# Turning the triangular blocks of a chunked delta-rule scan: products with the identity on TensorE in place of stream transposes on VectorE

## The chip, the cores and the metric

The kernel runs on one core of one Trainium2 chip. The metric is the device time of one launch in microseconds (us). Beside it stands the span of a profiled launch, from its first to its last instruction. TensorE (PE) runs at 2.4 GHz or at 1.2 GHz, as the chip grants; the profile shows the share granted, 1.00 or 0.50, or a mean of the two over a stretch.

## The reference

Two token streams (128 context tokens, 512 latent tokens) pass through two layers with shared weights. A layer mixes tokens in three ways, merges the three by gates, and ends in a feed-forward block. The change concerns one of the three, a chunked gated delta rule with 8 heads, a forward and a backward scan, and chunks of 64 tokens:

```python
    decay = jnp.exp(jnp.where(incl, gc[..., :, None] - gc[..., None, :], -jnp.inf))
    kb = k * beta[..., None]
    a_low = jnp.where(strict, jnp.einsum('bhnid,bhnjd->bhnij', kb, k) * decay, 0.0)
    m = a_low + jnp.eye(CHUNK, dtype=a_low.dtype)
    u = lax.linalg.triangular_solve(m, v * beta[..., None], left_side=True, lower=True, unit_diagonal=True)
    w = lax.linalg.triangular_solve(m, kb * jnp.exp(gc)[..., None], left_side=True, lower=True, unit_diagonal=True)
    ...
    def step(s, inp):
        u_n, w_n, qk_n, qg_n, kg_n, gl_n = inp
        v_new = u_n - jnp.einsum('bhcd,bhde->bhce', w_n, s)
        o = jnp.einsum('bhcd,bhde->bhce', qg_n, s) + jnp.einsum('bhij,bhje->bhie', qk_n, v_new)
        s = s * gl_n[..., None, None] + jnp.einsum('bhcd,bhce->bhde', kg_n, v_new)
        return s, o
```

Each chunk of each head and direction has a unit triangular 64x64 matrix `m`. The kernel inverts these matrices; the inverse then serves every product of the scan.

## The kernel before

**Data.** Activations lie transposed: channels on the 128 partitions, the 640 tokens along the row. The dense layers are *wide products*, 128x128 by 128x320. A float32 weight is split into a rounded part and a rest, and so are the activations, so that each 128x128 block of weights gives three products, written to a PSUM tile `pg`.

**Order of the work.** A recording layer writes one fixed order of instructions for each engine. The dense layers are the foreground. Everything else is a coroutine (`bg`), and `pump` (line 427), called between groups of wide products, steps those whose next work is due by an estimated clock that `tick` (line 365) keeps for each engine. A `yield` ends a step; its value says how many us ahead of its data a step may be issued. `finish_one` (line 448) steps a coroutine when the foreground has to wait for it. On the chip each engine then keeps to its order: an instruction that waits holds up everything behind it on its engine.

**The scans.** `delta` (line 1426) works on *units*: one chunk pair of 128 tokens, 8 heads, one direction in each half of the partitions. There are three sets of units for each layer (`batches`, line 1432): a *mixed* set of two units with both directions in each half (the context tokens), and two *plain* sets of four units (the latent tokens, directions 0 and 1). For each set, `prep` (line 1443) makes the matrices (`delta_unit`, line 1192: the decay from GpSimd and ScalarE, then 32 products of 64x64 for each unit on TensorE, and four VectorE multiplications) and inverts them (`delta_inv`, line 1229). Then `scan` (line 1465) runs the set's units one after another (`delta_step`, line 1346).

**The inverse** (`delta_inv`). `N`, seen as `Nm[partition, matrix, column]`, holds up to 32 matrices of 64x64 in each half of the partitions. Each matrix has two triangular 32x32 diagonal blocks, so the 128 partitions are four *quads* of 32 (`p` the half, `a` the block in it). In four parts:

- forward turn (`pack`, line 1244): from matrix layout (partition = row, and the 32 matrices side by side) to row layout in `U` (partition = matrix, and the 32x32 block along the row). A VectorE stream transpose turns 32 blocks of 32x32 of one quad; 4 for a plain set. In the mixed set the two directions need different layouts, so each quad is turned in both and the two are added, which takes 8 and one addition.
- the *substitution loop* (line 1265): 31 steps, on VectorE alone, 110 multiplications and subtractions that bring the inverse of all blocks into `X`.
- back turn (`unpack`, line 1279): `X` to matrix layout, back into `N` and, for one block of each matrix, the transposed block into `B`. 6 stream transposes for a plain set, 8 and 12 small copies for the mixed set.
- the off-diagonal block (from line 1305): two rounds of 32x32 products on TensorE, ScalarE takes their results out of PSUM.

`ident` is a 128x128 identity in the tile `small`. PSUM tiles `ps` (line 335) come from a pool of five. The tiles that the order and the rows call `A` are a shared pool: `N`, `U`, `X` and `B` are parts of `A` tiles.

Of the kernel before, what the change touches and what calls it, by code (L numbers as in the profile page):

```python
# [13 lines left out]
ALU = mybir.AluOpType  # L14
# [284 lines left out]
class _Net:  # L299
# [929 lines left out]
    def delta_inv(self, N, us):  # L1229

        nc = self.nc
        v = nc.vector
        nu = len(us)
        mixed = len(set(us)) > 1
        Nm = N.rearrange("p u c i -> p (u c) i")
        S = self.A()
        U = S[:, 0:1024].rearrange("p (r c) -> p r c", c=32)
        X = S[:, 1024:2048].rearrange("p (r c) -> p r c", c=32)
        tmp = S[:, 2048:2560]
        nc.gpsimd.memset(S[:, 1024:2048], 0.0)  # L1240
        nc.gpsimd.memset(S[:, 1024:2048].rearrange("p (r c) -> p r c", c=32).rearrange("p r c -> p (r c)")[:, 0:1024:33], 1.0)
        quads = [(p, a) for p in range(2) for a in range(2)]

        def pack(dst, p, a, bwd):
            q = slice(64 * p + 32 * a, 64 * p + 32 * a + 32)
            src = Nm[q, :, 32 * a:32 * a + 32].rearrange("p m i -> p i m")
            d = dst[q] if bwd else dst[q].rearrange("p r c -> p c r")
            v.transpose(out=d, in_=src)

        if not mixed:  # L1250
            for p, a in quads:
                pack(U, p, a, p ^ us[0])
                yield 1.5
        else:
            U2 = X
            for p, a in quads:
                pack(U, p, a, 0)
                yield 1.5
                pack(U2, p, a, 1)
                yield 1.5  # L1260
            v.tensor_tensor(out=U, in0=U, in1=U2, op=ALU.add)
            nc.gpsimd.memset(S[:, 1024:2048], 0.0)
            nc.gpsimd.memset(S[:, 1024:2048][:, 0:1024:33], 1.0)
        yield 1.5
        for c in range(31, 0, -1):
            js = [(c, 32)] if c > 24 else [(c, c + (32 - c) // 2), (c + (32 - c) // 2, 32)]
            tv = []
            for a, b in js:
                w = b - a
                tv.append(tmp[:, 256 * len(tv):256 * len(tv) + c * w].rearrange("p (r c) -> p r c", c=w))  # L1270
                v.tensor_tensor(out=tv[-1], in0=U[:, 0:c, c:c + 1].to_broadcast([P, c, w]),
                                in1=X[:, c:c + 1, a:b].to_broadcast([P, c, w]), op=ALU.mult)
            for (a, b), t in zip(js, tv):
                v.tensor_tensor(out=X[:, 0:c, a:b], in0=X[:, 0:c, a:b], in1=t, op=ALU.subtract)
            if c % 2 == 0:
                yield 1.5
        B = S[:, 0:1024].rearrange("p (m c) -> p m c", c=32)

        def unpack(dst, p, a, o2):
            q = slice(64 * p + 32 * a, 64 * p + 32 * a + 32)  # L1280
            src = X[q].rearrange("p r c -> p c r") if not o2 else X[q]
            v.transpose(out=dst.rearrange("p m i -> p i m"), in_=src)

        for p, a in quads:
            q = slice(64 * p + 32 * a, 64 * p + 32 * a + 32)
            bwd = p ^ us[0]
            nd = Nm[q, :, 32 * a:32 * a + 32]
            if mixed:
                unpack(nd, p, a, 0)
                yield 1.5  # L1290
                unpack(B[q], p, a, 1)
                ub = [u for u in range(nu) if p ^ us[u]][0]
                b3 = X[q, 0:8]
                bv, nv = B[q, ub * 8:ub * 8 + 8], nd[:, ub * 8:ub * 8 + 8]
                v.tensor_copy(b3, nv)
                v.tensor_copy(nv, bv)
                v.tensor_copy(bv, b3)
            else:
                unpack(nd, p, a, bwd)
                if a == bwd:  # L1300
                    yield 1.5
                    unpack(B[q], p, a, 1 - bwd)
            yield 0 if (p, a) == quads[-1] else 1.5

        W = S[:, 1024:2048].rearrange("p (m c) -> p m c", c=32)
        for m0 in range(0, nu * 8, 16):
            ps = self.ps()
            for m in range(m0, m0 + 16):
                s = us[m // 8]
                for p in range(2):  # L1310
                    fi = p ^ s
                    q0 = 64 * p + 32 * fi
                    q1 = 64 * p + 32 * (1 - fi)
                    nc.tensor.matmul(ps[q1:q1 + 32, (m - m0) * 32:(m - m0) * 32 + 32],
                                     Nm[q0:q0 + 32, m, 32 * (1 - fi):32 * (1 - fi) + 32], B[q0:q0 + 32, m],
                                     start=True, stop=True)
            for mm in range(m0, m0 + 16, 8 if mixed else 16):
                n = 8 if mixed else 16
                s = us[mm // 8]
                for p in range(2):  # L1320
                    q1 = 64 * p + 32 * (1 - (p ^ s))
                    nc.scalar.copy(W[q1:q1 + 32, mm:mm + n].rearrange("p m c -> p (m c)"),
                                   ps[q1:q1 + 32, (mm - m0) * 32:(mm - m0 + n) * 32])
        yield
        for m0 in range(0, nu * 8, 16):
            ps = self.ps()
            for m in range(m0, m0 + 16):
                s = us[m // 8]
                for p in range(2):
                    fi = p ^ s  # L1330
                    q0 = 64 * p + 32 * fi
                    q1 = 64 * p + 32 * (1 - fi)
                    nc.tensor.matmul(ps[q0:q0 + 32, (m - m0) * 32:(m - m0) * 32 + 32], W[q1:q1 + 32, m],
                                     Nm[q1:q1 + 32, m, 32 * (1 - fi):32 * (1 - fi) + 32], start=True, stop=True)
            for mm in range(m0, m0 + 16, 8 if mixed else 16):
                n = 8 if mixed else 16
                s = us[mm // 8]
                for p in range(2):
                    fi = p ^ s
                    q0 = 64 * p + 32 * fi  # L1340
                    nc.scalar.activation(Nm[q0:q0 + 32, mm:mm + n, 32 * (1 - fi):32 * (1 - fi) + 32],
                                         ps[q0:q0 + 32, (mm - m0) * 32:(mm - m0 + n) * 32].rearrange(
                                             "p (m c) -> p m c", c=32), AF.Copy, scale=-1.0)
        yield
# [857 lines left out]
```

## Time and profile before

| | us |
|---|---|
| time, median of 3 runs (lowest, highest) | 2847.31 (2843.88, 2851.53) |
| the profiled launch: its time | 2847.94 |
| its span | 2846.2 |
| TensorE busy | 2595.5 (91%) |
| VectorE (DVE) busy | 1870.7 (66%) |
| ScalarE (ACT) busy | 1030.8 (36%) |
| GpSimd (POOL) busy | 1331.2 (47%) |

The scans of layer 0 lie at about 290 to 610 us of the span, those of layer 1 at about 1690 to 2000 us. The busy shares are means over stages with different limits, so a stage is read by its own window. "Busy" of TensorE counts a product from its start to its modelled end; a product that runs at 1.2 GHz, or one that runs alone, counts for longer. The rate of a run of products is therefore read from the spacing of their starts. A float32 product stands as two matmul records in the trace.

### The profile page before, as it was taken

To read this page: it belongs to the slowest core of one execution; us is meant where nothing else is said; L and a number is where in the kernel's file an instruction comes from. 1 tells how busy PE (TensorE), PEld (TensorE's weight loads), DVE (VectorE), ACT (ScalarE), POOL (GpSimd) and SP (SyncE) were. 2 spreads that over 40 slices of the span, in tenths; PEclk is the share of its full clock that TensorE was granted. 3 is DMA by queue.
4 is the path that set the end of the run, shared out by engine and by line. 5 is a ranking of instruction groups with operands and counts; after the bars stand their busy time and mean duration, and the time that the engine had idled before them with its cause. 6 is when DMAs were issued, how large, how long until landed. Compare 5 with 4: busy or idle time off the path is not lost. (4 is left out here: it accounts for less than half of the span.)

```text
span 2846.2 us, 56258 instructions
## 1 busy us (share of the span) xinstructions
PE 2595.5 (91%) x22664; PEld 2455.5 (86%) x22664; DVE 1870.7 (66%) x3504; ACT 1030.8 (36%) x2235; POOL 1331.2 (47%) x1228
## 2 busy tenths in 40 slices
PE   5798879898999999999988988799899999999998
PEld 3677778898999989999987777688889989999997
DVE  4466897844654585667765779876556457877765
ACT  2445223332233243344425542333323323444432
POOL 1242535333334465566633444354423345767662
PEclk9899989999999999999999999899999999999999
DMA  7432122243564336422222322213336442222222
GB/s 277 165 99 93 61 85 66 78 139 120 186 241 135 112 98 202 139 83 82 82 99 80 108 85 72 78 57 97 109 140 232 157 163 62 73 82 82 82 75 82
DMA packets 99957, 324.24 MB, mean 114 GB/s; under 512 B 10842, under 2 KB 25178, under 8 KB 93216
## 3 DMA queue, kind: packets, MB, share of 16 engines
q1 hardware_dynamic: 98256, 312.76, 33.2%
q0 software_dynamic: 1440, 7.87, 0.8%
q8 instruction: 179, 2.93, 0.4%
q14 instruction: 82, 0.67, 0.1%
HBM read 288.60 MB, written 37.24 MB: 114 GB/s over the span
## 5 line engine op out<-in xcount | busy, mean ns | idle before, releaser
L2151 PE MATMUL pg<-A,wh 128*128 128x320 f32 (+1 forms) x6304 | 1477.1, 321 | 53.7 <-DVE T L2151 14.8
L2151 PEld LDWEIGHTS pg<-A,wh 128*128 128x128 f32 (+1 forms) x6304 | 1081.6, 194 | 107.5 <-issue 22.3
L2151 POOL TENSOR_TENSOR wl<-wr,wh 128x512 fp32r<-128x512 f32 (+2 forms) x486 | 677.5, 1407 | 777.5 <-ACT wh L2151 745.4
L2151 PE MATMUL pg<-A,wl 128*128 128x320 f32 (+1 forms) x3152 | 997.9, 317 | 0.5 <-POOL wl L2151 0.4
L2151 PEld LDWEIGHTS pg<-A,wl 128*128 128x128 f32 (+1 forms) x3152 | 610.7, 194 | 3.6 <-POOL wl L2151 2.6
L2151 ACT CAST wh<-wr 128x512 fp32r<-128x512 f32 (+2 forms) x486 | 286.7, 612 | 416.1 <-PE pg L2151 306.7
L2151 PE MATMUL ps<-A,wh 128*128 128x320 f32 x1696 | 379.6, 310 | 0.0
L2151 PEld LDWEIGHTS ps<-A,wh 128*128 128x128 f32 x1696 | 283.4, 188 | 3.4 <-issue 2.4
L2151 PE MATMUL ps<-A,wl 128*128 128x320 f32 x848 | 263.6, 311 | 4.6 <-POOL wl L2151 4.3
L2151 PE MATMUL ps<-A,A 32*32 32x32 f32 (+5 forms) x2984 | 214.0, 249 | 51.7 <-DVE A L2151 50.0
L2151 POOL TENSOR_TENSOR wl<-U,wh 128x512 fp32r<-128x512 f32 x160 | 225.9, 1425 | 52.9 <-ACT wh L2151 52.9
L2151 PEld LDWEIGHTS ps<-A,A 32*32 32x32 f32 (+2 forms) x2984 | 185.4, 152 | 63.8 <-DVE A L2151 51.2
L2151 DVE TENSOR_TENSOR A<-A 128x120 f32<-128x120 f32 (+22 forms) x690 | 215.6, 376 | 10.5 <-DMA A<-hyS 7.6
L2151 DVE TENSOR_TENSOR T<-T,T 128x320 f32<-128x320 f32 (+1 forms) x139 | 133.4, 960 | 100.6 <-ACT T L2151 96.4
L2151 POOL TENSOR_TENSOR A<-A,A 128x640 fp32r<-128x640 f32 (+5 forms) x84 | 121.4, 1457 | 113.3 <-ACT A L2151 110.0
L2151 PE MATMUL pg<-A,A 128*128 128x320 f32 x1056 | 164.6, 313 | 6.2 <-ACT A L2151 5.7
L2151 PEld LDWEIGHTS ps<-A,wl 128*128 128x128 f32 x848 | 159.6, 188 | 7.2 <-POOL wl L2151 7.2
L2151 PEld LDWEIGHTS pg<-A,A 128*128 128x128 f32 x1056 | 158.0, 190 | 8.5 <-ACT A L2151 6.0
L2151 ACT CAST wh<-U 128x512 fp32r<-128x512 f32 x160 | 99.1, 621 | 153.8 <-PE pg L2151 59.9
L2151 DVE STREAM_TRANSPOSE A<-A 32x1024 f32<-32x1024 f32 x72 | 149.0, 2093 | 1.3
L2151 DVE TENSOR_TENSOR U<-ps,U 128x512 f32<-128x512 f32 x144 | 78.1, 543 | 102.9 <-PE ps L2151 64.7
L2151 POOL TENSOR_TENSOR A<-U,A 128x320 fp32r<-128x320 f32 (+1 forms) x48 | 53.8, 1127 | 165.1 <-ACT A L2151 165.1
(166 smaller groups left out, 3120.1 us busy)
## 6 DMA issues: line engine op xcount, KB each, us to landing
wr<-in_wbig_dram SPq DMA_DIRECT2D x272, 512.0 KB, 3.7
A<-in_wmod_dram SPq DMA_DIRECT2D x96, 512.0 KB, 4.4
A<-hT SPq DMA_DIRECT2D x32, 1024.0 KB, 8.7
kSp<-U SPq DMA_DIRECT2D x40, 256.0 KB, 2.1
U<-kSp SPq DMA_DIRECT2D x40, 256.0 KB, 9.1
hyS<-T SPq DMA_DIRECT2D x24, 320.5 KB, 3.1
wr<-in_wbig_dram SPq DMA_DIRECT2D x16, 384.0 KB, 3.1
T<-hyS SPq DMA_DIRECT2D x16, 320.5 KB, 5.7
```

Of the source, the lines that this page charges most:

```text
L2151: return f(*a, **k)
```

## The change

In `delta_inv` every stream transpose becomes a group of float32 products on TensorE. The stationary operand is one strided column of `Nm` (32 matrices, 256 bytes apart) or one row or column of `X` (contiguous, or 128 bytes apart), the moving operand is the 32x32 identity of the quad, and the result, the block turned, lands in PSUM. ScalarE copies it from there to `U`, to `N` or to `B`. The four quads' products stand one after another, each on its own 32x32 block of TensorE.

- Plain set: forward 2 x 64 products and 4 copies; back 2 x (64 + 32) products and 12 copies.
- Mixed set: forward 2 x 64 products and 2 copies, and VectorE adds the second layout straight from PSUM in two halves; back 256 + 128 products with 8 moving columns and 8 copies. The 12 small VectorE copies and the second clearing of `X` on GpSimd go.
- The `yield 1.5` between the transposes go; a bare `yield` stands behind each group of products.

```diff
+        turn = lambda out, x, q, n: nc.tensor.matmul(out, x, self.ident[q, n], start=True, stop=True)
...
-            src = Nm[q, :, 32 * a:32 * a + 32].rearrange("p m i -> p i m")
-            d = dst[q] if bwd else dst[q].rearrange("p r c -> p c r")
-            v.transpose(out=d, in_=src)
...
-            v.tensor_tensor(out=U, in0=U, in1=U2, op=ALU.add)
-            nc.gpsimd.memset(S[:, 1024:2048], 0.0)
-            nc.gpsimd.memset(S[:, 1024:2048][:, 0:1024:33], 1.0)
+        for i0 in (0, 16):
+            ps = self.ps()
+            for i in range(16):
+                for p, a, q in quads:
+                    turn(ps[q, 32 * i:32 * i + 32], Nm[q, :, 32 * a + i0 + i], q, q)
+            v3 = ps.rearrange("p (i j) -> p i j", j=32)
+            if mixed:
+                nc.scalar.copy(U[:, i0:i0 + 16], v3)
+            else:
+                for p in range(2):
+                    h = slice(64 * p, 64 * p + 64)
+                    d = U[h, i0:i0 + 16] if p ^ us[0] else U[h, :, i0:i0 + 16].rearrange("p r c -> p c r")
+                    nc.scalar.copy(d, v3[h])
+            pss.append((i0, v3))
+            yield
+        if mixed:
+            for i0, v3 in pss:
+                d = U[:, :, i0:i0 + 16].rearrange("p r c -> p c r")
+                v.tensor_tensor(out=d, in0=d, in1=v3, op=ALU.add)
...
-            v.transpose(out=dst.rearrange("p m i -> p i m"), in_=src)
...
+                for i in range(ni):
+                    for p, a, q in quads:
+                        for u in range(nu) if mixed else (0, ):
+                            bwd = p ^ us[u]
+                            if o2 and a != bwd:
+                                continue
+                            m = slice(8 * u, 8 * u + 8) if mixed else slice(0, 32)
+                            x = X[q, i0 + i] if bwd ^ o2 else X[q, :, i0 + i]
+                            turn(v3[q, i, m], x, q, slice(q.start + m.start, q.start + m.stop))
...
+                    nc.scalar.copy(d.rearrange("p m i -> p i m"), v3[q, :, m])
+                yield
```

**VectorE, layer 0, start of the mixed set's inverse.** `A_2453` holds `N`, `A_2682` holds `U` and `X` of the mixed set; `A_2692` and `A_2693` belong to the first plain set. Before:

```order
L2151 TENSOR_TENSOR A_2453<-ps_2632,A_2453 128x256
L2151 STREAM_TRANSPOSE A_2682<-A_2453 32x32x32
L2151 STREAM_TRANSPOSE A_2682<-A_2453 32x1024
L2151 STREAM_TRANSPOSE A_2682<-A_2453 32x32x32
L2151 STREAM_TRANSPOSE A_2682<-A_2453 32x1024
L2151 STREAM_TRANSPOSE A_2682<-A_2453 32x32x32
L2151 STREAM_TRANSPOSE A_2682<-A_2453 32x1024
L2151 STREAM_TRANSPOSE A_2682<-A_2453 32x32x32
L2151 STREAM_TRANSPOSE A_2682<-A_2453 32x1024
L2151 TENSOR_TENSOR A_2682<-A_2682 128x1024
L2151 TENSOR_TENSOR A_2693<-ps_2788,A_2692 128x256
```

Now:

```order
L2157 TENSOR_TENSOR A_2453<-ps_2632,A_2453 128x256
L2157 TENSOR_TENSOR A_2682<-A_2682,ps_2685 128x16x32
L2157 TENSOR_TENSOR A_2682<-A_2682,ps_2769 128x16x32
L2157 TENSOR_TENSOR A_2682<-A_2682 128x31 x2
L2157 TENSOR_TENSOR A_2682<-A_2682 128x60
```

The eight transposes and the long addition are gone. Two additions that read PSUM stand in front of the substitution loop (the last two rows), and they need the products and copies of the two other engines first.

**TensorE, layer 0, end of the mixed set's inverse.** `ps_3869` is the first round of 32x32 products for the off-diagonal block, the first TensorE instruction that needs the substitution loop. Before:

```order
L2151 MATMUL pg_3862<-A_465,wh_3716 128x320
L2151 MATMUL pg_3862<-A_463,wl_3717 128x320
L2151 MATMUL ps_3869<-A_2682,A_2453 32x32 x32
L2151 MATMUL pg_3862<-A_463,wh_3716 128x320
L2151 MATMUL pg_3862<-A_465,wh_3716 128x320
```

Now the first that needs it are the 256 products of the back turn:

```order
L2157 MATMUL pg_3597<-A_465,wh_3440 128x320
L2157 MATMUL pg_3597<-A_463,wl_3441 128x320
L2157 MATMUL ps_3604<-small,A_2682 32x8 x256
L2157 MATMUL pg_3597<-A_463,wh_3440 128x320
L2157 MATMUL pg_3597<-A_465,wh_3440 128x320
```

Before, 534 wide products stand between the mixed set's units and `ps_3869`. Now 240 stand between its units and `ps_3604`, 228 of them behind the first group of forward turns. Wide products have moved from ahead of the inverse to behind it: up to the end of the last set's inverse there are 1778 before and 1610 now.

## Rows read from the trace of the kernel before

**Rows 1.** Windows: layer 0's and layer 1's inverses, then layer 0's three parts.
```profile
core 0: us, PE busy (x) PEld busy (x) DVE busy (x) ACT busy (x) POOL busy (x), PEclk, DMA share, GB/s
294.76:565.40 270.64, 227.40 (x3135) 215.04 (x3133) 234.64 (x481) 82.81 (x197) 121.79 (x151) 0.89 0.22 68
1693.07:1958.94 265.87, 223.88 (x3134) 212.04 (x3133) 232.04 (x481) 80.49 (x195) 125.30 (x148) 0.90 0.23 70
...
294.76:413.49 118.73, 90.66 (x790) 86.42 (x789) 116.53 (x241) 28.85 (x67) 50.67 (x65) 0.90 0.23 73
413.49:495.60 82.11, 76.17 (x1553) 70.11 (x1554) 56.94 (x104) 32.49 (x83) 47.23 (x60) 0.87 0.21 63
495.60:565.40 69.80, 60.56 (x793) 58.51 (x792) 61.17 (x138) 21.47 (x48) 23.89 (x26) 0.90 0.21 67
```

**Rows 2.** Groups of VectorE and TensorE, 294.76:565.40 (busy, mean ns | idle before <-releaser).
```profile
L2151 DVE TENSOR_TENSOR A<-A 128x126 f32<-128x126 f32 (+24 forms) x331 | 92.1, 342 | 1.5
L2151 DVE STREAM_TRANSPOSE A<-A 32x1024 f32<-32x1024 f32 x36 | 74.4, 2092 | 0.7
L2151 DVE SCALAR_TENSOR_TENSOR T<-T,par,T 128x641 f32<-128x641 f32 x24 | 30.0, 1251 | 16.1 <-POOL wl L2151 6.4 <-POOL A L2151 4.8 <-issue 4.3
L2151 DVE TENSOR_TENSOR A<-ps,A 128x256 f32<-128x256 f32 x32 | 12.7, 420 | 0.8 <-PE ps L2151 0.3
L2151 DVE COPY A<-A 32x256 f32<-32x256 f32 x12 | 4.5, 379 | 0.4
...
L2151 PE MATMUL pg<-A,wh 128*128 128x320 f32 x714 | 170.6, 328 | 8.9 <-DVE T L2151 8.8
L2151 PE MATMUL ps<-A 64*64 64x64 f32 x448 | 16.5, 224 | 4.0 <-DVE A L2151 3.0 <-DVE S L2151 1.1
L2151 PE MATMUL ps<-A,A 32*32 32x32 f32 x640 | 16.4, 222 | 24.4 <-DVE A L2151 24.4
L2151 PE MATMUL ps<-U,stcr 128*128 128x512 f32 x16 | 6.1, 450 | 5.9 <-POOL U L2151 5.9
```

**Rows 3.** Order in time on VectorE, then on TensorE (start, us, what, [idle before <-releaser]).
```profile
294.76 16.52 DVE L2151 STREAM_TRANSPOSE A<-A 32x1024 f32<-32x1024 f32 x8
311.31 1.23 DVE L2151 TENSOR_TENSOR A<-A 128x1024 f32<-128x1024 f32 x1
...
413.49 0.32 PE L2151 MATMUL ps<-A,A 32*32 32x32 f32 x4 [13.29 <-DVE A L2151]
551.57 0.31 PE L2151 MATMUL ps<-A,A 32*32 32x32 f32 x2 [4.81 <-DVE A L2151]
```

**Rows 4.** Windows behind those two waits.
```profile
413.49:422.00 8.51, 8.51 (x144) 8.05 (x145) 5.87 (x26) 3.57 (x9) 0.89 (x1) 0.50 0.33 102
550.00:565.40 15.40, 10.18 (x269) 9.61 (x269) 7.62 (x4) 4.94 (x9) 3.51 (x4) 0.56 0.01 2
```

**Rows 5.** Runs of products: start, us from first start to last end, records.
```profile
1858.40 2.21 PE L2151 MATMUL ps<-A,A 32*32 32x32 f32 x128
482.86 1.15 PE L2151 MATMUL ps<-A 64*64 64x64 f32 x32
1863.38 1.16 PE L2151 MATMUL ps<-S,A 64*64 64x64 f32 x64
2464.36 1.76 PE ps L2151 x12
```

**Rows 6.** Groups of the whole span: copies from PSUM, PSUM reads, clearings of X.
```profile
L2151 ACT COPY U<-ps 128x512 f32<-128x512 f32 x54 | 31.8, 595 | 27.1 <-PE ps L2151 25.8 <-POOL A L2151 0.8 <-POOL wl L2151 0.3
L2151 DVE TENSOR_TENSOR U<-ps,A 128x512 f32<-128x512 f32 x40 | 26.8, 683 | 10.4 <-PE ps L2151 10.3
L2151 POOL MEMSET A<- 128x1024 f32 x10 | 9.5, 951 | 17.3 <-DVE A L2151 17.3
L2151 ACT COPY A<-ps 32x512 f32<-32x512 f32 x16 | 9.2, 576 | 35.4 <-PE ps L2151 35.2
```

More of the change, by code (lines that the diff above doesn't have):

```diff
@@ L1241, in delta_inv @@
         nc.gpsimd.memset(S[:, 1024:2048].rearrange("p (r c) -> p r c", c=32).rearrange("p r c -> p (r c)")[:, 0:1024:33], 1.0)
-        quads = [(p, a) for p in range(2) for a in range(2)]
-        def pack(dst, p, a, bwd):
-            q = slice(64 * p + 32 * a, 64 * p + 32 * a + 32)
-            src = Nm[q, :, 32 * a:32 * a + 32].rearrange("p m i -> p i m")
-            d = dst[q] if bwd else dst[q].rearrange("p r c -> p c r")
-            v.transpose(out=d, in_=src)
[L1250 to L1260, printed above, removed]
-            v.tensor_tensor(out=U, in0=U, in1=U2, op=ALU.add)
-            nc.gpsimd.memset(S[:, 1024:2048], 0.0)
-            nc.gpsimd.memset(S[:, 1024:2048][:, 0:1024:33], 1.0)
+        quads = [(p, a, slice(64 * p + 32 * a, 64 * p + 32 * a + 32)) for p in range(2) for a in range(2)]
+        turn = lambda out, x, q, n: nc.tensor.matmul(out, x, self.ident[q, n], start=True, stop=True)
+        pss = []
+        for i0 in (0, 16):
[17 more added lines that the diff above has]
+                v.tensor_tensor(out=d, in0=d, in1=v3, op=ALU.add)
         yield 1.5
@@ L1277, in delta_inv @@
         B = S[:, 0:1024].rearrange("p (m c) -> p m c", c=32)
-        def unpack(dst, p, a, o2):
-            q = slice(64 * p + 32 * a, 64 * p + 32 * a + 32)
-            src = X[q].rearrange("p r c -> p c r") if not o2 else X[q]
-            v.transpose(out=dst.rearrange("p m i -> p i m"), in_=src)
[L1284 to L1303, printed above, removed]
+        yield
@@ new lines, in delta_inv @@
+        n = 16 if mixed else 32
+        for i0 in range(0, 32, 512 // n):
+            ni = 512 // n
+            for o2 in range(2):
+                ps = self.ps()
+                v3 = ps.rearrange("p (i m) -> p i m", m=n)
+                used = []
+                for i in range(ni):
[7 more added lines that the diff above has]
+                            turn(v3[q, i, m], x, q, slice(q.start + m.start, q.start + m.stop))
+                            if not i:
+                                used.append((a, q, m))
+                for a, q, m in used:
+                    if o2:
+                        d = B[q, m, i0:i0 + ni]
+                    elif mixed and m.start:
+                        continue
+                    else:
+                        m = slice(0, n)
+                        d = Nm[q, m, 32 * a + i0:32 * a + i0 + ni]
+                    nc.scalar.copy(d.rearrange("p m i -> p i m"), v3[q, :, m])
+                yield
```

## The prediction

> **What bounds the kernel now.** I read the page's busy shares first, then windows of the two places where the changed code runs, then the groups of VectorE and TensorE in them, then the order in time around TensorE's longest waits.
>
> The whole span is TensorE's (91% busy), but not where the change lies. From the mixed set's forward turn to the end of the last set's inverse, layer 0 takes 270.64 us: VectorE is busy for 234.64 and TensorE for 227.40, so TensorE is idle for 43.24. Layer 1: 265.87, 232.04, 223.88, idle 41.99 [rows 1]. In the first part (294.76 to 413.49) VectorE is busy for 116.53 of 118.73 us, TensorE for 90.66: this part is VectorE's. The second part is nearer TensorE's (76.17 of 82.11), the third is VectorE's again (61.17 of 69.80) until its last transpose.
>
> The groups say on what: 331 small multiplications and subtractions, which are the three substitution loops (3 x 110, and one addition), 92.1 us, or 0.278 each and 30.6 for one loop; 36 stream transposes, 74.4 us, 2.07 each; 12 small copies, 4.5 [rows 2]. TensorE's idle time is put down to the same: 24.4 us before the 32x32 products, 8.8 before wide products whose PSUM tile VectorE had not read, 3.0 and 1.1 inside the scans, 5.9 before products that wait for GpSimd [rows 2]. The two longest single waits are 13.29 and 4.81 us, both for VectorE [rows 3], and behind them TensorE works at 1.2 GHz: a granted share of 0.50 and 0.56 [rows 4]. A transpose is not the only thing they wait for: the substitution loop before it is, too.
>
> **What goes.** Per layer 36 transposes (74.4 us), 12 copies (4.5) and the long addition (1.23 [rows 3]), 80 us of VectorE. New on VectorE are two additions of 512 columns from PSUM, 0.68 each [rows 6]. VectorE falls from 235 to 156 us in this stretch, and TensorE's 227 becomes the larger number. So the gain is no longer bounded by what VectorE loses, but by TensorE's idle time, 43 and 42 us.
>
> **What is added on TensorE.** Per layer 2 x 320 products for the plain sets and 512 for the mixed one, 1152, twice as many records. No run of before turns a block this way, so its price has to be bounded. The 32x32 products of the off-diagonal block use two 32x32 blocks of TensorE by turns: 128 records in 2.21 us, less the last one's own 0.2, is 15.8 ns each at 2.4 GHz, or 31.5 for each block [rows 2, 5]. Do four blocks run beside each other? The 64x64 products answer for their size: 32 records on two blocks take 1.15 us, 64 records on four blocks take 1.16 [rows 5], twice the rate. By that a product of the change (two records, a quarter of the time of its block) costs 15.8 ns. Of the 1152, 1024 stand on four blocks and 128 (the `B` blocks of the plain sets) on two: 1024 x 15.8 + 128 x 31.5 = 20.2 us. With the fill of some fourteen short groups I take 21 us per layer. From above: if each product had TensorE to itself, 63 ns, 73 us per layer. From below, nothing, if they fell wholly into time that TensorE waits anyway. I take the value near the first, since the nearest rows (same size, same type) carry it.
>
> One thing in it is shown by no row: the stationary operand is read at a step of 128 or 256 bytes. "SBUF — State Buffer" of the Trainium skill (Door 1: The DMA port swizzle) says that SBUF is read in lines of 16 bytes and that each access to a new line pays. No run here shows a weight load at such a step; the stream transposes write at the same steps in half of their forms and all take 2.1 us, but that is VectorE. If a weight load became the longer part of a record, the price moves towards the upper bound.
>
> **What is added on ScalarE.** Per layer 2 x 16 + 10 copies at 0.58 us [rows 6], 24 us. It is busy for 82.81 of 270.64 us [rows 1], so there is room in sum. On the path stand two copies ahead of the mixed loop, and the last copies ahead of each set's 32x32 products, with 12 wide products between on TensorE as cover. I cost them in the waits below.
>
> **Which waits stay.** The loop is untouched, and TensorE's order now has products in front of it and behind it. For the mixed set of layer 0, between the second group of forward turns and the back turn, TensorE has about 41 us: 228 wide products less 6, at 0.147 (12 in 1.76 us [rows 5]), 32.6; four units' 128 products of 64x64 at 0.030, 3.8; 8 with `stcr`, about 2; 128 turns, 2. VectorE has the loop (30.6), the first 12 steps of the next set's loop (3.3), 16 multiplications of units at 0.40 (6.4 [rows 2]), some small ones (1.4) and the two additions (1.4), 43 us, and starts about 4 us later: two groups of turns, a copy, and a semaphore each. So TensorE waits some 5 us, plus 2 before the forward turn (the units' last multiplications) and 2 for GpSimd. That last one was 5.66 here; it shrinks, because the second clearing of `X` is gone, in which GpSimd waited for VectorE ahead of those units [rows 6]. 9 in all, where this part has 28 now [rows 1]. The first plain set's loop is covered by the scan steps and back turns, some 2 us stay. In the second plain set TensorE has 41 us between forward and back turn (234 wide products and the mixed scan's rest), VectorE the loop and four convolutions (30.6 + 8 x 1.25 [rows 2]), and the handover of 3: about 4 us. The waits inside the scans stay, 2.6. Together 18 us of idle time in each layer against 43 and 42: 25 and 24 come back.
>
> **The clock.** Behind the two long waits TensorE ran for 8.5 us at half rate and 10.2 busy us at about half [rows 4]: some 9 us lost. With waits of 5 us in place of 13 I give back 5.
>
> **Sum.** Layer 0: -25 - 5 + 21 = -9; layer 1: -24 - 5 + 21 = -8. From the profiled launch, 2847.9, that gives 2831; the median lies 0.6 us under it, so 2830. What the other 1150 wide products of the stage do is unchanged; the 168 that move behind the inverse cost the same there.
>
> **Rivals.**
>
> 1. *The turns cost more than the idle time that they free* (slower). TensorE is the bound of the kernel, so each us of turns that is not in a wait is a us of time. The point from which it decides: 25 + 5 us come back per layer, so 1152 products may cost 26 ns each. For it: the strided weight load, the 8-column groups of the mixed set, which take the same block twice running (384 of 1152 products), and rows only for contiguous operands. At 35 ns, twice the price, each layer adds 40 in place of 21: 2830 + 38 = 2868. One at a time, 73 per layer: 2934. The Trainium skill has a rule on this side: "VectorE: DVE Perf Modes" (Rules for kernel authors) calls VectorE's transpose the fastest for 32x32 blocks. By rows, one transpose of 32 blocks is 2.07 us [rows 2], and 32 products on four blocks with their copy are 0.5 + 0.58: the rule holds only if the products run one at a time (2.0 + 0.58). Chance of this rival 0.15.
> 2. *The waits only move* (slower). The order was laid by estimates that are too short for VectorE (`tick` books a transpose at 1.15 us, the trace has 2.07 [rows 2]), so TensorE may stand before the back turn as long as it stood before the 32x32 products; the two waits then keep their 13 and 5 us and the low clock. Idle falls by the 10 us that do not hang on the loop: -10 + 21 = +11 a layer, 2869 with nothing from the clock. Against it: VectorE has 80 us less to do. Chance 0.08.
> 3. *Idle goes wholly and the clock stays high*: -43 - 9 + 21 = -31 and -42 - 9 + 21 = -30, 2787. Against it: the loops alone are 92 us of VectorE in a row of waits. Chance 0.12 for near this.
> 4. *The two sides cancel*: waits of 25 to 30 us stay in each layer, and the time is within 0.3%. Chance 0.20.
>
> That the change does not do what it says (no transposes removed, or other work moved in) is excluded by the order.
>
> **Chances and range.** The forecast has 0.45. 0.3% of the time, 8.5 us, is about what a measurement of this kernel can tell from no change. Faster by more than that: the forecast and rival 3, 0.57. Within: rival 4, 0.20. Slower: rivals 1 and 2, 0.23. The forecast's own range, with the turns between 18 and 25 us and the waits between 12 and 22 per layer, is 2812 to 2842. The range for 8 in 10 reaches down towards rival 3, to 2795, and up past rivals 1 and 2, to 2876; the one-at-a-time case is left out.
>
> **What would show it.** No stream transpose in VectorE's groups, and VectorE busy near 156 us in the stretch from the first group of turns to the last 32x32 products. A group of 64 turns as 128 records in 1.2 us at 2.4 GHz: if it takes 2.2, only two blocks ran together; if over 4, one. TensorE idle near 18 us in that stretch, with its longest wait before the mixed set's back turn, near 5 us, on VectorE. Copies `A<-ps` of 32x512 on ScalarE near 0.58 us: over 1 us, the strided write costs. The stretch should end 25 to 45 us earlier, with 168 fewer wide products in it. The forecast is wrong if records of turns are spaced at over 13 ns, or if TensorE's wait before the back turns is as long as before.

## The result, and the profile after

| | before | after |
|---|---|---|
| time, median (lowest, highest), us | 2847.93 (2843.88, 2851.53) | 2893.16 (2890.1, 2902.8) |
| ratio of after to before | | 1.0159, 95% interval 1.0138 to 1.018 |
| span of the profiled launch | 2846.2 | 2891.9 |
| TensorE busy | 2595.5 | 2664.5 |
| VectorE busy | 1870.7 | 1715.0 |
| ScalarE busy | 1030.8 | 1110.4 |

The change makes the kernel 45 us slower; the forecast was 2830, 63 us less. VectorE lost 156 us and TensorE gained 69 busy us. All of it is in the two scan stages, so I read those first. A stage here goes from the first `stcr` product of a layer's units to the first product of the stage after the scans; it holds the same 1350 (layer 0) and 1302 (layer 1) wide products in both kernels. Windows of the two stages before:

```profile
core 0: us, PE busy (x) PEld busy (x) DVE busy (x) ACT busy (x) POOL busy (x), PEclk, DMA share, GB/s
284.10:628.55 344.45, 297.95 (x4378) 280.87 (x4376) 260.68 (x545) 111.80 (x264) 157.22 (x185) 0.92 0.26 83
1685.14:2015.19 330.05, 284.83 (x4249) 267.36 (x4247) 259.11 (x541) 104.88 (x253) 158.25 (x180) 0.92 0.25 78
```

and after, with the two stretches that answer to [rows 1], from the first group of turns to the last 32x32 product:

```profile
283.21:648.21 365.00, 332.75 (x6682) 311.88 (x6680) 185.38 (x498) 150.46 (x306) 156.01 (x183) 0.94 0.25 80
1707.87:2064.17 356.30, 323.50 (x6552) 303.57 (x6551) 181.59 (x494) 145.25 (x295) 152.51 (x178) 0.94 0.23 73
293.98:558.39 264.41, 235.21 (x5270) 221.15 (x5269) 160.16 (x434) 114.31 (x224) 111.14 (x141) 0.92 0.22 68
1715.93:1985.00 269.07, 239.67 (x5282) 225.54 (x5281) 156.19 (x434) 115.29 (x225) 113.82 (x142) 0.92 0.22 68
```

The stages are 20.5 and 26.3 us longer, together 46.8; the span grew by 45.7. Idle time of TensorE (length less busy) falls by 14 and 13 us, from 46.5 and 45.2 to 32.3 and 32.8. Busy time rises by 35 and 39. The groups of TensorE and ScalarE in layer 0's stage say with what (the columns are those of [rows 2]); layer 1's busy times are the same within 0.2 us:

```profile
L2157 PE MATMUL ps<-small,A 32*32 32x32 f32 x1536 | 28.8, 217 | 17.3 <-DVE A L2157 16.8 <-issue 0.5
L2157 PE MATMUL ps<-small,A 32*32 32x8 f32 x768 | 12.0, 194 | 9.3 <-issue 6.2 <-DVE A L2157 3.0
L2157 ACT COPY A<-ps 32x512 f32<-32x512 f32 x36 | 34.1, 946 | 29.9 <-PE ps L2157 29.5
L2157 ACT COPY A<-ps 64x512 f32<-64x512 f32 x8 | 6.6, 823 | 23.7 <-PE ps L2157 23.7
```

The turns (`ps<-small,A`) are 28.8 + 12.0 = 40.8 us where the forecast had 21. In front of them stand 6.7 us (0.5 and 6.2) of a kind that TensorE did not have in these stages before: "issue", time in which it waited for nothing that the profile shows. The copies of 32x512 take 0.95 us in the mean, not 0.58 [rows 6]; 8 of the 36 belong to the off-diagonal block and stay at 0.58, so that a copy of the turns takes about 1.05. TensorE's waits in layer 0's stretch (us in total, times, the longest):

```profile
PE ps L2157 <- DVE A L2157: 20.4, 6, 9.4
PE ps L2157 <- issue: 6.8, 5, 2.1
PE ps L2157 <- ACT A L2157: 1.8, 3, 0.8
```

In layer 1 they are 18.8, 8.6 and 1.8. TensorE in order of time, the wait ahead of the first plain set's forward turn, the mixed set's back turn, and the first plain set's:

```profile
336.58 2.05 PE L2157 MATMUL ps<-small,A 32*32 32x32 f32 x128 [9.36 <-DVE A L2157]
...
359.40 3.19 PE L2157 MATMUL ps<-small,A 32*32 32x8 f32 x220 [3.04 <-DVE A L2157]
364.14 1.95 PE L2157 MATMUL ps<-small,A 32*32 32x8 f32 x128 [1.55 <-issue]
367.59 1.95 PE L2157 MATMUL ps<-small,A 32*32 32x8 f32 x128 [1.51 <-issue]
371.60 0.66 PE L2157 MATMUL ps<-small,A 32*32 32x8 f32 x34 [2.06 <-issue]
...
419.03 2.00 PE L2157 MATMUL ps<-small,A 32*32 32x32 f32 x64
422.93 2.00 PE L2157 MATMUL ps<-small,A 32*32 32x32 f32 x128
427.70 2.00 PE L2157 MATMUL ps<-small,A 32*32 32x32 f32 x64
```

128 records take 2.0 us on four quads, and 64 records on two quads (the `B` groups) take 2.0 as well. So every quad works beside the others, but one block needs 125 ns for a product, where the off-diagonal products of [rows 5] need 69 (2.21 us for 64 products on two blocks that alternate). VectorE meanwhile:

```profile
378.24 0.49 DVE L2157 SCALAR_TENSOR_TENSOR T<-T,pg 128x320 f32<-128x320 f32 x1 [17.07 <-ACT T L2157]
```

It stands for 17 us behind TensorE's long row of turns, because its next instruction works on a wide product's PSUM tile and on ScalarE's part of it, and both come only after the row; the next set's loop is queued behind it.

### The profile page after: what moved, and what is told of

Read it like the earlier page. It is cut to its first block, busy times and chain, and to the rows that moved or that the text cites. A ratio compares the mean times of both kernels' runs of the same rounds, so it can differ in the third digit from the quotient of the medians.

```text
span 2891.9 us, 65462 instructions
## 1 busy us (share of the span) xinstructions
PE 2664.5 (92%) x27272; PEld 2520.5 (87%) x27272; DVE 1715.0 (59%) x3410; ACT 1110.4 (38%) x2319; POOL 1324.3 (46%) x1224
## 5 line engine op out<-in xcount | busy, mean ns | idle before, releaser
L2157 DVE TENSOR_TENSOR A<-A 128x120 f32<-128x120 f32 (+20 forms) x688 | 215.7, 377 | 10.8 <-DMA A<-hyS 8.1
L2157 PE MATMUL ps<-A,A 32*32 32x32 f32 (+5 forms) x2984 | 206.1, 238 | 5.9 <-ACT A L2157 3.6
L2157 PEld LDWEIGHTS ps<-A,A 32*32 32x32 f32 (+2 forms) x2984 | 178.0, 141 | 17.7 <-ACT A L2157 5.1
L2157 ACT COPY A<-ps 32x512 f32<-32x512 f32 (+6 forms) x184 | 122.1, 679 | 164.1 <-PE ps L2157 153.2
L2157 PE MATMUL ps<-small,A 32*32 32x32 f32 (+2 forms) x4848 | 120.2, 215 | 67.7 <-DVE A L2157 43.1
L2157 PEld LDWEIGHTS ps<-small,A 32*32 32x32 f32 (+1 forms) x4848 | 108.0, 138 | 80.3 <-issue 41.0
```

Source lines behind the costliest of these rows:

```text
L2157: return f(*a, **k)
```

## The experiments

Every ratio is to runs of the kernel before on the same chip.

**The turn by itself, and the copies.** One product of the burst, its operand and its step:

```python
x = data[q, 0:32 * step].rearrange("p (m s) -> p s m", s=step)[:, i % step]
nc.tensor.matmul(v[o, i], x, ident[q, q], start=True, stop=True)
```

> A kernel of its own that computes nothing of the reference: bursts of 64 turns, each behind 16 wide products, with the step of the stationary operand, the number of quads, the column group and the type changed one at a time; then 512-column copies from PSUM with steps on either side. In the changed kernel 128 records of turns take 2.04 us on four quads and 64 records on two quads 2.01. Step theory (a block's weight load at a step of 128 or 256 bytes takes twice as long): contiguous stationary gives 128 records in 1.2 us or less, steps of 128 and 256 bytes 2.0; somewhere between 4 and 128 bytes it turns. Array theory (blocks whose row group and column group are the same, or four float32 products, do not run abreast): contiguous is 2.0 too, and a shifted column group or fewer quads changes the rate. Copies: 0.58 us contiguous; written at a step of 128 or 256 bytes near 1.05 us; read from PSUM at a step and written in runs unknown, 0.58 to 1.05. Two long bursts of 384 turns: if the gaps of 1 to 2 us in the mixed back turn belong to the length of a burst, they show here too; if they come from traffic or from what else the kernel does, they do not.

TensorE, bursts in order: on four quads at steps of 256, 128, 16, 8 and 4 bytes; on two quads at 4 and at 128; on four quads with PSUM written at a step of 64 bytes (stationary contiguous); and the start of the row of 384 turns, which is strided (128 bytes):

```profile
17.69 2.04 PE L80 MATMUL s<-ident,data 32*32 32x32 f32 x128
23.51 2.02 PE L80 MATMUL s<-ident,data 32*32 32x32 f32 x128
...
41.09 2.12 PE L80 MATMUL s<-ident,data 32*32 32x32 f32 x128
46.99 1.29 PE L80 MATMUL s<-ident,data 32*32 32x32 f32 x128
52.09 1.29 PE L80 MATMUL s<-ident,data 32*32 32x32 f32 x128
57.15 2.21 PE L80 MATMUL s<-ident,data 32*32 32x32 f32 x128
...
68.12 3.82 PE L80 MATMUL s<-ident,data 32*32 32x32 f32 x128
...
118.47 1.29 PE L80 MATMUL s<-ident,data 32*32 32x32 f32 x128
...
129.34 3.17 PE L80 MATMUL s<-ident,data 32*32 32x8 f32 x207
133.56 2.03 PE L80 MATMUL s<-ident,data 32*32 32x8 f32 x128 [1.05 <-issue]
137.01 2.03 PE L80 MATMUL s<-ident,data 32*32 32x8 f32 x128 [1.42 <-issue]
140.74 2.04 PE L80 MATMUL s<-ident,data 32*32 32x8 f32 x128 [1.70 <-issue]
```

The step theory holds and the array theory falls: four quads run side by side (1.29 us for 128 records, 8.6 ns each, where 1.2 or less was expected), another column group changes nothing (1.29 and 2.02), and only the step costs. At 4 and 8 bytes nothing, from 16 bytes on 2.0 to 2.2 us, a factor of 1.6 to 1.7. "SBUF — State Buffer" of the Trainium skill (Door 1: The DMA port swizzle) says that SBUF is read in lines of 16 bytes and wants two hits in a line; the run agrees with that, since a step of 8 bytes is the last that hits a line twice. It does not agree with what the passage there derives from it, that 4 float32 are the step that is still free: at 16 bytes, which is 4 float32, the burst takes 2.12 us.

The second finding is the long row: after 207 records come 1.05 to 1.70 us of nothing before each further 128, so that a turn in a long row costs 54 to 58 ns. Contiguous turns in a long row of the next run cost the same (each 128 records start 3.46 and 3.73 us apart there), though at a granted share of 0.50, where their records are no faster. The trace shows what the gaps go with. While the row runs, the DMA moves nothing but one packet of 16 KB, of the queue that carries instructions, for each further 128 records. Every gap ends a near constant time after such a packet's start: 2.3 to 2.6 us in the ten gaps of the two long rows here, 2.3 to 2.7 us in ten gaps of the changed kernel. The queue in the whole run (packets, MB, share), and the row around two of these packets (the last column is GB/s):

```profile
q8 instruction: 32, 0.52, 1.0%
...
131.30:134.50 3.20, 2.15 (x150) 2.05 (x146) 0.00 (x0) 0.00 (x0) 0.00 (x0) 0.55 0.00 0
134.50:134.70 0.20, 0.20 (x28) 0.20 (x25) 0.00 (x0) 0.00 (x0) 0.00 (x0) 0.50 0.29 82
134.70:138.10 3.40, 1.98 (x138) 1.89 (x136) 0.00 (x0) 0.00 (x0) 0.00 (x0) 0.50 0.00 0
138.10:138.30 0.20, 0.20 (x28) 0.20 (x26) 0.00 (x0) 0.00 (x0) 0.00 (x0) 0.50 0.39 82
```

The copies on ScalarE (contiguous; written at a step of 128 bytes; PSUM read at a step and SBUF written in runs):

```profile
188.93 0.57 ACT L126 COPY data<-s 32x512 f32<-32x512 f32 x1 [4.95 <-DVE data L131]
189.54 1.00 ACT L127 COPY data<-s 32x512 f32<-32x512 f32 x1
...
191.60 0.57 ACT L129 COPY data<-s 32x512 f32<-32x512 f32 x1
```

**Contiguous operands in place.**

```diff
-turn(ps[q, 32 * i:32 * i + 32], Nm[q, :, 32 * a + i0 + i], q, q)
+turn(ps[q, 32 * i:32 * i + 32], Nm[q, i0 + i, 32 * a:32 * a + 32], q, q)
-x = X[q, i0 + i] if bwd ^ o2 else X[q, :, i0 + i]
+x = X[q, i0 + i]
```

> The changed kernel with one thing other: every turn reads its stationary operand as 32 neighbouring floats instead of 32 floats at a step of 128 or 256 bytes. The order of all instructions and their number stay; the turned values are wrong. Step theory: records of turns fall from 16 to about 8 ns (from 31 to 16 in the groups on two quads), 1152 products per layer from 41 to about 20 us, so 40 us in all: near 2853. Array theory: the rate stays and the time too, 2893.

2871.3 us (1.0076, 1.0061 to 1.0091): 22 us of the 40 expected. The groups show why:

```profile
L2206 PE MATMUL ps<-small,A 32*32 32x32 f32 x1536 | 20.1, 199 | 11.9 <-DVE A L2206 10.0 <-issue 1.9
L2206 PE MATMUL ps<-small,A 32*32 32x8 f32 x768 | 9.4, 183 | 8.8 <-issue 7.4 <-DVE A L2206 1.4
```

The plain sets' turns and the forward turns fall by 8.7 us. The mixed back turn falls by 2.6. It stays a long row, with 7.4 us of gaps, and where the clock stands at 0.50 contiguous turns need 15 ns a record again (128 in 1.94 us). The turns are 29.5 and 30.1 us in the two layers, against 40.8 and 40.7. So the step is about half of the 45 us, and not all of them; the time lies between the two theories' 2853 and 2893.

**One part alone.** The mixed set, the plain sets, or the forward turn of all sets by TensorE, the rest by the stream transposes of before:

```diff
+FWD_PE, BACK_PE = ("mixed",), ("mixed",)
 ...
+if kind not in FWD_PE:
+    ...    # pack() as before
+else:
+    ...    # products
```

> Turns by TensorE in the mixed set alone; the plain sets keep the stream transposes of before. By the trace of the changed kernel the mixed set's turns are 4 us forward and 12 back with 6 to 8 us of gaps between them, against 28 us of idle time in this part before: if turn price and idle time simply add in each part, the time is within 10 us of before (2840 to 2855). If the plain sets' relief is what pays for the mixed set's turns, it comes out near 2875 or above.

> Turns by TensorE in the two plain sets alone; the mixed set keeps its stream transposes and copies. The plain sets' turns are 24 us of TensorE per layer in the changed kernel, and TensorE had 4 and 9 us of idle time there before: if both simply add, 12 to 18 us per layer are lost, 2872 to 2885. If the plain sets' turns lie in idle time, it stays near 2848.

> Only the forward turn by TensorE, in all three sets; the back turn is the stream transposes and copies of before. TensorE gets 384 turns per layer, 12.3 us at 32 ns; VectorE loses 16 transposes and the long addition, 34 us. No burst is longer than 64 turns, so no gaps. If TensorE's idle time falls with VectorE's load as the prediction had it (some 25 us for 80 us of VectorE), 10 to 15 us per layer come back and the time is within 6 us of before, 2842 to 2854. If idle time doesn't follow VectorE's load but the order of waits, 24 us are added: near 2870.

| run | time, us | ratio to before (95%) | TensorE idle in the two stages, us |
|---|---|---|---|
| before | 2847 to 2850 | 1 | 46.5, 45.2 |
| mixed set alone | 2878.7 | 1.0111 (1.0087 to 1.0136) | 48.1, 45.4 |
| plain sets alone | 2869.9 | 1.0068 (1.0053 to 1.0083) | 35.8, 42.2 |
| forward turn alone | 2861.1 | 1.0047 (1.0032 to 1.0063) | 43.3, 36.6 |
| the change | 2893.2 | 1.0159 (1.0138 to 1.018) | 32.3, 32.8 |

The plain sets came out 2 us under the range written for them (2872 to 2885), so price and idle time nearly add there. The mixed set did not come out within 10 us of before: it takes 30 and 36 us of busy time from VectorE in the two layers and leaves TensorE's idle time where it was. The forward turn alone lies between its two ranges (2842 to 2854, near 2870): 3.2 and 8.6 us of idle time come back for 12.7 and 12.6 us of turns, so idle time follows VectorE's load only in part. VectorE stands still for 16.9 us while the long row runs (no releaser is shown here; in the trace of the change it is ScalarE's part of a wide product's tile),

```profile
380.54 0.49 DVE L2206 SCALAR_TENSOR_TENSOR T<-T,pg 128x320 f32<-128x320 f32 x1 [16.90 <-issue]
```

and ahead of the first plain set's 32x32 products TensorE then waits 11.0 us in this run, 2.67 in the trace of before. That the one leads to the other is argued, not shown.

**The long row cut up, and fewer turns.** A `yield` after every eight columns; then also one product of 16 columns in each form in place of 8-column products, from which the copies pick:

```diff
+                        if mixed and i % 8 == 7 and i < ni - 1:
+                            yield
```
```diff
+for form in range(2):
+    for i in range(32):
+        for p, a, q in quads:
+            x = X[q, i] if form else X[q, :, i]
+            turn(v3[q, i], x, q, slice(q.start, q.start + 16))
+        if i % 8 == 7 and i < 31:
+            yield
```

> The changed kernel with the mixed set's back turn cut up: after every eight columns the coroutine gives way, so that 6 or more wide products stand between pieces of 64 or 32 turns, where the changed kernel issues 256 and 128 in one go. The number of turns and copies stays. Supply theory (TensorE runs dry of instructions in long rows of small products; the row of 768 records took 19.5 us standing alone, 25.5 ns a record, where 128 take 14.2 each): the gaps of 6.3 and 7.8 us per layer go, VectorE no longer stands idle for 17 us in there, since wide products keep it fed, and the time falls by 14 to 30 us, to 2863 to 2879. Rival (the gaps are only where the work waits for copies or for PSUM, and come back elsewhere): within 5 us of 2893.

> As the run before with cut pieces, and the mixed back turn with 256 turns of 16 columns in place of 384 of 8: each block is turned once in either form, and the copies pick from the two. Pieces of 32 turns with 6 wide products between. If a turn costs what its weight load at a step costs (32 ns on four quads), 128 turns fewer per layer are 4 us per layer: 8 us below the run with pieces of 64 and 32. If the pieces' own starts cost, no gain.

The first gave 2887.5 us (1.014, 1.0114 to 1.0166), not the 2863 to 2879 expected: no difference from the change that these intervals can tell. The gaps did go (from 6.8 and 8.6 to 1.4 and 1.9 us), idle time fell to 28.1 and 24.9 us, and busy time rose by 3.4 and 1.9. In the stretch of the cut-up row TensorE is at a mean granted share of 0.69:

```profile
357.00:385.00 28.00, 26.40 (x823) 24.14 (x824) 18.61 (x88) 6.75 (x9) 4.72 (x4) 0.69 0.21 65
```

The wide products that fill the gaps run at half rate there until about 377 us. The second gave 2877.0 (1.0106, 1.0078 to 1.0134), 10.5 less than the first where 8 were expected. The two intervals overlap; the trace bears it out with turns of 37.4 and 37.7 us in place of 41.8 and 41.4.

**The mixed set alone, repaired; then later.** The 256 turns above, and the copies with the loops the other way; in the second run one number:

```diff
-nc.scalar.copy(d.rearrange("p m i -> p i m"), v3[q, :, m])
+nc.scalar.copy(d, v3[q, :, m].rearrange("p i m -> p m i"))
```
```diff
-            yield
+            yield -4.0
```

> Mixed set alone by TensorE, with 256 turns of 16 columns in pieces of 32, and the copies out of PSUM read at a step and written in runs (0.58 us where the other way is 1.0). Plain sets as before. Per layer 128 + 256 turns, 12.3 us on TensorE, against 37 us of VectorE. The set alone as the change has it gave 2879, 29 over before. Supply theory: without long rows the 8 us of gaps per layer and VectorE's idle time behind them go, and 4 us of turns: 2840 to 2858. If the mixed set's relief is worth nothing anyway, because what VectorE does next is the longer chain: 2870.

> As the run with the mixed set alone, 256 turns in pieces of 32, with one number changed: the back turn may be issued only 4 us after the estimate of its data, so that 24 more wide products stand ahead of it. In that run TensorE waited 3.0 us ahead of the back turn and was then at a granted share of 0.50 through six of the eight pieces and the wide products between them (6 in 1.83 us, 0.9 at full clock). Clock theory: with the wait gone the clock stays at 1.00 through the pieces; 3 us of waiting and some 7 us of half-rate wide products go per layer, 2850 becomes 2828 to 2838, faster than both. Rival (the small products themselves bring the clock down, or the wait only moves): the pieces are at 0.50 again, and the time is 2843 to 2850.

2850.3 (1.0011, 0.9998 to 1.0023) and 2841.0 us (0.9978, 0.9969 to 0.9988). The first is in the supply theory's range (2840 to 2858) and not to be told from before; the second lies between its two ranges. The pieces of the back turn in layer 0, first run and second:

```profile
360.40:377.50 17.10, 17.10 (x421) 15.03 (x420) 12.39 (x57) 1.05 (x2) 2.08 (x2) 0.51 0.15 53
```
```profile
361.40:376.00 14.60, 14.58 (x547) 12.90 (x548) 14.29 (x53) 1.57 (x3) 7.72 (x8) 1.00 0.20 65
```

With the wait ahead of them cut from 3.0 to 1.2 us, the clock stays at 1.00, and more work is done in less time. In layer 1, behind a wait of 1.3 us, four pieces are still at 0.50, so the length of the wait alone does not decide it. And part of the gain moved: TensorE now waits 9.4 us ahead of the first plain set's 32x32 products, 4.6 in the run before. Each theory is borne out in part.

**The copies alone in the changed kernel.** The first of the two edits above, and the same for the forward turn's copies.

> The changed kernel with the copies out of PSUM in the other order of loops: PSUM is read at a step and SBUF written in runs of 16 or 32 floats, where the changed kernel reads in runs and writes at steps of 128 or 256 bytes. By the copies measured alone, 0.57 us in place of 1.00, some 36 copies per layer, 15 us of ScalarE. On the path stand the last copies ahead of each loop and of each set's 32x32 products. If they count there: 2 to 4 us per layer, 2885 to 2889. If TensorE's wide products cover them: 2893.

2888.0 us (1.0143, 1.0123 to 1.0163). The copies fell from 946 to 577 ns:

```profile
L2206 ACT COPY A<-ps 32x512 f32<-32x512 f32 x36 | 20.8, 577 | 35.8 <-PE ps L2206 35.4
```

The time is 5 us under that of the change and in the range of "they count there", but the intervals of the two overlap: the copies are at most a small part.

**The order alone.** A wait that later wide products can cover is removed by issuing the waiting products later. Once without any turn by TensorE, once with the mixed set's:

```diff
-yield 0 if (p, a) == quads[-1] else 1.5
+yield (-12.0 if mixed else -8.0) if (p, a) == quads[-1] else 1.5
```
```diff
-            yield -4.0
+            yield -6.0
-yield 0 if (p, a, q) == quads[-1] else 1.5
+yield (-12.0 if mixed else -8.0) if (p, a, q) == quads[-1] else 1.5
```

> The kernel before, stream transposes and all, with one expression other: the off-diagonal products of the mixed set may be issued only 12 us after the estimate of their data, those of a plain set 8 us after it, so that 90 more wide products stand ahead of the mixed set's. Theory that the idle time is a matter of order (a wait of 13.3 us ahead of the mixed set's 32x32 products that later wide products can cover): the wait falls to 1 or 2 us, the low clock behind it goes, 10 to 18 us per layer: 2815 to 2830, more than any version with turns gave. Rival (VectorE's chain through the three sets is the bound in this stretch, so that the time only moves to the next wait, ahead of the first plain set): within 5 us of 2848.

> The mixed set alone by TensorE as in the run with the later back turn, with the back turn 6 us after the estimate in place of 4 (layer 1 still had a wait of 1.3 us and half clock there) and the plain sets' off-diagonal products 8 us after it (waits of 9.4, 5.9 and 3.7 us in layer 0, 2.6, 5.0 and 3.7 in layer 1). If the waits can be covered by order: 6 to 12 us per layer off 2841, 2817 to 2829, and against the kernel before with the same late products it shows what the turns themselves are worth. If VectorE's chain is the bound: 2836 to 2841.

The kernel before with later 32x32 products: 2833.1 us (0.9952, 0.9936 to 0.9967), 3 us above the range of its theory. The long wait is gone, but one of 11.6 us appears in layer 1 ahead of the scan's 64x64 products, on VectorE, and TensorE is still idle for 37.4 and 41.1 us in the two stages; the rival has a part in it. The mixed set by TensorE, held in the same way: 2800.5 (0.9829, 0.9811 to 0.9847), the best of all, 17 us under its range and 33 us under the former. The former had one choice of delays, this one the second of two, so the 33 us are the turns' worth at these delays and not at the best of each. Its two stages:

```profile
285.29:606.97 321.68, 300.24 (x5145) 280.55 (x5144) 229.40 (x518) 115.41 (x278) 164.05 (x183) 0.98 0.27 90
1665.79:1970.85 305.06, 286.81 (x5017) 267.98 (x5015) 224.19 (x514) 110.88 (x267) 162.05 (x178) 0.99 0.25 85
```

Idle 21.4 and 18.3 us, and busy 2 us above before, although 12.0 us of turns are in it: the clock (0.98 and 0.99, before 0.92) gave back the rest, 3.8 us of it on the wide products and 4.5 and 4.8 on the off-diagonal block.

**All sets, later; all sets, repaired and later.** Back turns 6 us late, plain forward turns 8 us late, in the changed kernel and in the one with 256 mixed turns in pieces and the cheaper copies.

```diff
-            yield
+            yield -6.0
+            if not mixed:
+                yield -8.0
             pss = []
```

> The changed kernel, every turn by TensorE, long row and all, with back turns issued 6 us and the plain sets' forward turns 8 us after the estimate of their data. If the order was the fault (waits of 19.6 and 17 us in the two layers, at half clock behind them), these go as they went in the mixed-only kernel (41 us): 2850 to 2865. If the price of the turns is the fault (41 us of products and 7 of gaps per layer, where 43 us were idle), the gaps and the low clock of the long row stay: 2870 to 2885.

> All sets by TensorE with every repair found: 256 mixed turns in pieces of 32, copies written in runs, back turns 6 us and plain forward turns 8 us late. Against the mixed-only kernel with the same repairs (2800) it shows what the plain sets' turns cost: 640 products per layer, 24 us of TensorE by the spacing of 32 ns on four quads and 63 on two. If TensorE's time is all that counts now: 2800 + 2 x 24 = 2848, less at most 10 per layer for idle time they fill: 2828 to 2848. If order was all: near 2800.

2868.8 (1.007, 1.0052 to 1.0089), between its two ranges, and 2835.3 us (0.9956, 0.9942 to 0.9969), as written for "TensorE's time is all that counts". The order was worth 24 us of the slowdown; with the change's own turns the kernel stays 19 us slower than before. The repaired one, its stages:

```profile
282.83:621.71 338.88, 324.47 (x6426) 303.21 (x6424) 181.99 (x498) 135.29 (x310) 155.55 (x183) 0.97 0.27 85
1679.08:2000.59 321.51, 310.02 (x6296) 290.29 (x6295) 182.98 (x494) 130.55 (x299) 155.45 (x178) 0.99 0.26 81
```

Against the mixed set alone it is 35 us longer: 24 and 23 busy us more per layer, the price of the plain sets' turns, of which only 7 come back as idle time.

## Why the prediction was wrong

**The step that failed: "a product of the change costs 15.8 ns", 21 us per layer.** Measured: 40.8 and 40.7 us. The concurrency that I argued from [rows 5] was right; the rows' contiguous operands were not those of the change. I named the step of the operand as shown by no row, gave the upper bound for it, and still took the lower value, "since the nearest rows (same size, same type) carry it". The operand's step is part of what makes a row near. The price as a whole is +39 us over the two layers, and the step is 22 of them, by the run with contiguous operands. The other 17 stay there (29.5 and 30.1 us against my 21). By the bursts, contiguous turns at full clock would be about 25 us, an estimate (16 groups of 128 records at 1.29 and 4 of 64 on two quads at 1.20): my "fill" was too small. The rest goes with the clock, which I had put at 2.4 GHz throughout: in a row at a granted share of 0.50, 128 contiguous records take 1.94 us.

**A term that was missing: rows of turns that outrun their supply.** "A group of 64 turns" was my unit, and the mixed back turn is 256 and 128 in one go. 6.8 and 8.6 us of gaps, +15 us. That the gaps come with the length of the row is shown (alone, and cut up). That it is the supply of instructions the traces bear out: one packet of instructions for each further 128 records, and the end of each gap 2.3 to 2.7 us behind a packet's start. No run changed the supply itself.

**The waits** were nearly right in sum: 18 forecast, 22.2 and 20.6 measured without the gaps (20.4 + 1.8, 18.8 + 1.8), +7 us. Their places were not: the longest is 9.36 us ahead of the plain set's forward turn, where I had 2; the mixed back turn's is 3.04, where I had 5.

**The clock** was to give back 5 us in each layer; beside the turns, busy time fell by 6.0 us in layer 0 and by 2.0 in layer 1 (34.8 and 38.7 more busy time, less the turns): +2. In both layers it is the off-diagonal products that got shorter (16.4 to 11.8 us and 15.9 to 11.9), while the wide ones gained nothing in layer 0 and lost 3.5 us in layer 1. What the forecast did not see is that turns behind a wait leave the clock low and the wide products between them pay.

**ScalarE's copies**, 0.58 us forecast, are about 1.05: "over 1 us, the strided write costs" is what happened, with little on the path.

In sum: -17 forecast, +39 +15 +7 +2 makes +46; measured 45. The forecast's own range was added up wrongly: with turns of 25 us and waits of 22 it ends at 2846, not 2842.

The rule of the Trainium skill that I had weighed there ("VectorE: DVE Perf Modes", Rules for kernel authors) calls VectorE's transpose the fastest for 32x32 blocks. By rows, 32 turns on four quads and their copy are 1.0 + 1.05 us against 2.07 for one transpose [rows 2]: in time a tie, but the 1.0 is on the engine that bounds the kernel, so the rule's side won for the change as it stands. It did not for the mixed set with its turns repaired and later, the fastest kernel here.

Of the rivals the first decided ("the turns cost more than the idle time that they free", break-even 26 ns, measured 32 on four quads and 63 on two, 35 in the mean: 40.8 us over 1152). Its price at 35 ns, 2868, lacked the gaps. The signs that I had named worked: 128 records in 2.0 us in place of 1.2. But one of them misled, "2.2, only two blocks ran together": the 2.0 us, near what two blocks would take, came from four slow ones. VectorE in the stretch is 160.2 and 156.2, forecast 156.

## What to carry to other kernels

Before work is moved to the engine that bounds the kernel, price it from a row with the same access pattern as well as the same size, count how many instructions it issues in one go, and look at what the other engine does while the bound one is busy with it. Idle time of the bound engine in a fixed order is in part a matter of order: here later products alone gained 14 us without any new work, though most of the idle time stayed. The mixed set's turns, which lost 29 us as a long row behind a wait, came out 33 us under that as 256 products in short pieces, with copies written in runs and issued later.

## What the hardware showed that I had not expected

- A stationary operand of 32 floats costs 1.6 to 1.7 times the contiguous one at each of the five steps tried from 16 to 256 bytes; 8 bytes cost nothing. In bfloat16 (32 elements 64 bytes apart) it is the same: 64 records in 1.09 us, contiguous 0.65.
- Strided turns take 2.0 us for 128 records at a granted clock of 0.50 as at 1.00; contiguous ones 1.94 us at 0.50 and 1.29 at 1.00.
- Writing PSUM at a step of 64 bytes costs TensorE nothing (1.29 us), and reading it at a step of 128 bytes costs ScalarE nothing (0.57); writing SBUF at a step of 128 bytes costs ScalarE 1.00 in place of 0.57.
- Where a row of small products outruns its instructions, TensorE stands: 20 gaps of 0.5 to 2.6 us, ten alone and ten in the changed kernel, all end 2.3 to 2.7 us after the start of a 16 KB packet of the instruction queue.
- The clock can fall in a long row of small products without a wait ahead: behind 16 wide products in a row, the granted share fell from 1.00 to 0.50 within the first 207 records of the row of 384 turns standing alone, before its first gap. In the second such row (32 columns) it fell only behind the first gap. The first from 131 us on, its gaps included:

```profile
131.00:149.10 18.10, 10.55 (x668) 10.05 (x661) 0.00 (x0) 0.00 (x0) 0.00 (x0) 0.52 0.02 5
```
